# First stage by feature tiles: scale and shift of a tile by partial products in four column quarters, eight output tiles side by side

## The chip, the core and the metric

The kernel runs on one core of a Trainium2 chip. The metric is the device time of one execution in microseconds (us); lower is better. The core has a matrix engine (TensorE: PE in the profile, with PEld for its weight loads), VectorE (DVE), ScalarE (ACT), GpSimd (POOL) and SyncE (SP), which issues the transfers here. Each engine works through its own instructions in order and waits for others by semaphores.

## The reference

Two transformer blocks in float32 for 256 tokens of 1024 features. What the change touches is the beginning of the first block: from the conditioning vectors `c` and `c_ctx` a scale and a shift of each of 1024 features are computed, the tokens `x` and the 256 context tokens `ctx` are normalised, scaled and shifted, and projected by `w_in`.

```python
mod_x = (silu(c) @ w_ada + b_ada)          # 6 parts of 1024: shift, scale, gain of the mixing and of the ffn
mod_c = silu(c_ctx) @ w_ada + b_ada
px = (rms_norm(x,   g_pre_mix) * (1 + sc_m)  + sh_m)  @ w_in
pc = (rms_norm(ctx, g_pre_mix) * (1 + csc_m) + csh_m) @ w_in
# px, pc are split into: attention q, k, v; mLSTM q, k, v, o and 16 gates
# then window attention with a sink, a two-way chunked mLSTM, w_out, residual, SwiGLU;
# a second block of the same size follows, and a last norm
```

## The kernel before, in words

**Layout.** Features lie on the 128 partitions, in KD = 8 feature tiles `k`; tokens lie along the free axis: 256 tokens of `x`, then 256 of `ctx`. A product in float32 is made of three matmuls on rounded halves (`mm3`, L443): high weights by high input, high by low, low by high. H and L are the halves of the weights, `self.xh` and `self.xl` those of the input.

**The weight stream.** `make_plan` (L216) lists all weight blocks of 128 by 128 (320 wide for the values, `v1`) in the order of use and packs them into items of up to 1024 columns. `load_raw` issues one transfer for each into six buffers `raw` (NRAW = 6, L331); a buffer is loaded anew when its item has been split. `prep_item` (L392) splits an item: ACT copies it to H (L399), DVE subtracts to get L (L400). Items of the kind "ada" hold rows of `w_ada` for the later gains; DVE multiplies them by `self.cbx`, the silu of `c` on all partitions (L406), so `cbx` must be there before the first of them. `block()` hands out the next block and keeps the splits LA = 3 items ahead; in the first stage it is 0, and the splits are called by hand.

**The first stage, `start` (L592).** Tokens are loaded, squared on ACT (L657) and summed over the features on DVE (L658); PE sums over the partitions (L527), DVE computes the row factors and lays them on a diagonal (L548), PE spreads them to all partitions (L556), ACT copies them to `R` (L560). The 16 transfers `araw` of 512 KB hold the part of `w_ada` that gives shifts and scales. Scales: `rows(h, i)` multiplies two feature tiles of `cs` (silu of both conditionings, 2 columns) with 512 columns (L673); `scales` turns the two rows into columns (L699) and DVE adds bias and gain (L702, L703). Shifts of tiles 0 to 5: `dots(k)` on DVE (L713) and POOL (L711), summed on ACT (L719); of tiles 6 and 7: `rows_f` (L682) and `shifts` (L692). `inp(k)` applies scale, shift and R to tile k (DVE L727, POOL L728 and L729, ACT L730 and L731), `low(k)` makes the low half (DVE L735, L737).

The run "gates" sends three output tiles of 512 columns (`held`: gates, and two of mLSTM keys) through the eight feature tiles side by side, and the table `hooks` calls `step(k)` and `ahead(k)` between its 24 blocks. Near its end `ahead(5)` issues loads 3 to 5 and beyond and the second part of `cst` (the rotation tables, L793).

**Behind it, `mix1` (L828).** Two tiles of mLSTM queries (`mq`), the attention keys (`ak`) and the first query tile (`aq0`) follow one output tile after another, each over all eight feature tiles; between them the steps of `ml_gates` (log-sigmoid on ACT at L938 to L940, scans on DVE from L943, transposes on PE at L990) are taken by `next(gates)`. Then come the values `v1`, token-major, in two halves of eight blocks; L990 stands between the halves. The string `MIX1` sets the order of what follows: `A` is a unit of attention, `c` of the context state, `q1` to `q3` and `o0` to `o3` are further projections, `a`/`b` the mLSTM heads. PSUM has 8 banks: 4 tagged "mm", 3 "at", 1 "sm".

## Time and profile before

| | |
|---|---|
| time, median of 3 runs | 1040.81 us |
| lowest and highest run | 1036.70 and 1040.88 us |
| span of the profiled execution | 1037.3 us |
| PE busy, share of the span | 994.6 us, 96% |
| DVE, ACT, POOL busy | 663.2, 495.8, 217.5 us |
| bytes moved | 175.56 MB, mean 169 GB/s |

Of the profiled execution its span is recorded, from its first to its last instruction, and no time beside it. Times below count from the start of that span. Busy PE time counts matmuls as they lie in the pipeline, one over the next, so 96% does not mean that PE streams columns 96% of the time.

### The profile page before, as it was taken

The page shows a single profiled execution, that of the slowest core. Times are in us where ns is not written, and L with a number is a line of the kernel's source. Part 1 is how long each engine was busy: PE and PEld are TensorE (multiplying, and loading weights), DVE is VectorE, ACT ScalarE, POOL GpSimd, SP SyncE. Part 2 cuts the span into 40 slices and gives each one's busy share as a digit, 9 for nine tenths or more (in the row PEclk, how much of TensorE's full clock was granted, in tenths as well). Part 3 has the DMA queues.
Part 4 walks back from the last instruction along what each step waited for, and adds up shares of the span by engine and source line. Part 5 has one row for each costly group of instructions (what it writes and reads, how often), then busy time and mean ns, then how long its engine had stood idle before and what let it go on. Part 6 is the DMA issues. An engine that isn't in the chain of part 4 may idle for free. (4 is left out here: it accounts for less than half of the span.)

```text
span 1037.3 us, 18663 instructions
## 1 busy us (share of the span) xinstructions
PE 994.6 (96%) x7500; PEld 917.4 (88%) x7500; DVE 663.2 (64%) x1154; ACT 495.8 (48%) x834; POOL 217.5 (21%) x220
## 2 busy tenths in 40 slices
PE   6899999988999999889999999999999999999996
PEld 2389767888999999789999999998779999999995
DVE  6779758877788744665555554554357866566543
ACT  4374555556544445354444343644355545444441
POOL 0831102360000001411111020115355421111000
PEclk9999999989999999889999999999999999999998
DMA  9665604454678655245555555353224555555531
GB/s 336 239 207 160 207 2 134 175 210 153 203 227 279 205 183 184 81 151 191 168 181 169 174 174 171 102 183 123 82 82 161 185 187 182 188 188 190 184 124 41
DMA packets 49514, 175.56 MB, mean 169 GB/s; under 512 B 5506, under 2 KB 6802, under 8 KB 49428
## 3 DMA queue, kind: packets, MB, share of 16 engines
q1 hardware_dynamic: 49428, 174.38, 50.3%
q8 instruction: 59, 0.97, 0.4%
q14 instruction: 27, 0.22, 0.1%
HBM read 173.30 MB, written 1.05 MB: 168 GB/s over the span
## 5 line engine op out<-in xcount | busy, mean ns | idle before, releaser
L400 DVE TENSOR_TENSOR L<-raw,H 128x1024 fp32r<-128x1024 f32 (+2 forms) x259 | 322.0, 1246 | 224.2 <-ACT H L399 224.0
L399 ACT ACTIVATE H<-raw 128x1024 fp32r<-128x1024 f32 (+2 forms) x278 | 289.7, 1048 | 203.6 <-PE mm L446 83.0
L446 PE MATMUL mm<-x,H 128*128 128x256 f32 (+3 forms) x1064 | 307.6, 289 | 3.9 <-DVE x L737 3.6
L445 PE MATMUL mm<-x,H 128*128 128x256 f32 (+3 forms) x1032 | 301.2, 292 | 3.4 <-ACT x L1249 3.4
L447 PE MATMUL mm<-x,L 128*128 128x256 f32 (+3 forms) x1032 | 297.3, 288 | 0.0
L446 PEld LDWEIGHTS mm<-x,H 128*128 128x128 f32 x1064 | 203.1, 191 | 7.8 <-DVE x L737 5.9
L445 PEld LDWEIGHTS mm<-x,H 128*128 128x128 f32 x1032 | 197.2, 191 | 11.1 <-ACT x L1249 4.8
L447 PEld LDWEIGHTS mm<-x,L 128*128 128x128 f32 x1032 | 196.9, 191 | 1.2
L447 PE MATMUL mm<-hh,L 128*128 128x256 f32 (+1 forms) x528 | 150.3, 285 | 0.0
L445 PE MATMUL mm<-hh,H 128*128 128x256 f32 (+1 forms) x528 | 149.7, 284 | 0.0
L446 PE MATMUL mm<-hl,H 128*128 128x256 f32 (+1 forms) x528 | 149.5, 283 | 0.0
L445 PE MATMUL at<-x,H 128*128 128x256 f32 (+2 forms) x472 | 135.4, 287 | 0.0
L447 PE MATMUL at<-x,L 128*128 128x256 f32 (+2 forms) x472 | 135.3, 287 | 0.0
L446 PE MATMUL at<-x,H 128*128 128x256 f32 (+2 forms) x472 | 135.3, 287 | 0.0
L445 PEld LDWEIGHTS mm<-hh,H 128*128 128x128 f32 x528 | 99.7, 189 | 0.0
L446 PEld LDWEIGHTS mm<-hl,H 128*128 128x128 f32 x528 | 99.5, 188 | 0.0
L447 PEld LDWEIGHTS mm<-hh,L 128*128 128x128 f32 x528 | 99.3, 188 | 0.0
L514 POOL TENSOR_TENSOR acc<-acc,t 128x256 f32<-128x256 f32 (+1 forms) x42 | 41.2, 980 | 238.4 <-ACT t L1206 177.2
L446 PEld LDWEIGHTS at<-x,H 128*128 128x128 f32 x472 | 90.4, 192 | 0.1
L445 PEld LDWEIGHTS at<-x,H 128*128 128x128 f32 x472 | 90.4, 192 | 0.1
L447 PEld LDWEIGHTS at<-x,L 128*128 128x128 f32 x472 | 90.5, 192 | 0.0
L1306 POOL TENSOR_TENSOR g<-g,R 128x272 f32<-128x272 f32 (+1 forms) x44 | 33.2, 758 | 216.7 <-ACT g L1305 216.7
(371 smaller groups left out, 1323.0 us busy)
## 6 DMA issues: line engine op xcount, KB each, us to landing
raw<-wst SPq DMA_DIRECT2D x298, 512.0 KB, 3.8
araw<-ada SPq DMA_DIRECT2D x16, 512.0 KB, 7.5
raw<-wst SPq DMA_DIRECT2D x8, 480.0 KB, 3.4
raw<-wst SPq DMA_DIRECT2D x4, 320.0 KB, 2.8
XT<-xin SPq DMA_DIRECT2D x2, 544.0 KB, 4.3
CT<-cin SPq DMA_DIRECT2D x2, 512.0 KB, 7.5
out<-XT SPq DMA_DIRECT2D x8, 128.0 KB, 2.0
cst<-cst SPq DMA_DIRECT2D x1, 392.0 KB, 4.1
```

The lines of the kernel that those rows point to most:

```text
L399: self.A.activation(H[:, :w], src, AF.Copy)
L400: low = lambda: (self.G if self.poolsplit else self.V).tensor_tensor(L[:, :w], src, H[:, :w].bitcast(F32), op=ALU.subtract)
L445: T.matmul(out, H, xh, start=start, stop=False)
L446: T.matmul(out, H, xl, start=False, stop=False)
L447: T.matmul(out, L, xh, start=False, stop=stop)
L514: self.G.tensor_tensor(st["acc"], st["acc"], sq, op=ALU.add)
L1306: G.tensor_tensor(g, g, R[:, :n], op=ALU.mult)
```

## The change

The first stage goes by feature tiles. One transfer `araw` (1 MB, four buffers) now holds, for feature tile k, the 128 columns of the scale and the 128 of the shift over all eight tiles of the contraction. `mod_rows(k)` multiplies it with `cs`, now 32 columns wide with the two conditionings in the first two: contraction tile j goes to output partitions 32 (j mod 4), so four partial sums grow in four column quarters of the array. ACT copies the 128 by 256 result to `row`. `mod_cols(k)` multiplies it by `sel`, which has ones where the partition modulo 32 is 0 or 1: this adds the quarters and turns rows to columns. `inp(k)` makes M, SH and both halves of the input on DVE and ACT; POOL has no part in it.

Eight output tiles go through the feature tiles side by side: gates, two of mLSTM keys and the attention keys with 512 columns (four "mm" banks), two of mLSTM queries and attention queries 0 and 1 with 256 (two "at" banks, two tiles in each). Query tile 1 thereby moves from `MIX1` to the first stage. `cbx` comes by a transfer that repeats one row for all partitions, and one silu on ACT, behind the stage. The rows of `w_ada` in the stream stand at other places (`ADA1`), as many as before, and the steps of `ml_gates` start with `v1`.

```diff
-    "A c c c q1 c a0 A q2 a1 b0 A a2 A b1 A a3 b2 q3 o0 b3 A t o1 A t t t t t o2 A m t A t k o3 A s"
+    "A c c c a0 A q2 c a1 b0 A a2 A b1 A a3 b2 q3 o0 b3 A t o1 A t t t t t o2 A m t A t k o3 A s"
-ADA1 = (1, 1, 1, 1, 1, 0, 0, 2, 1, 0, 2, 2, 1, 2, 0)
+ADA1 = (1, 1, 1, 1, 1, 1, 1, 1, 2, 2, 1, 2)
+FIRST = (W1_GATES, W1_MK, W1_MK + 128, W1_AK, W1_MQ, W1_MQ + 128, W1_AQ, W1_AQ + 128)
+    put("sel", np.stack([np.arange(128) % 32 == i for i in range(2)], 1).astype(np.float32))
-    add("gates", together([g[:8], g[8:16], g[16:]]))
-    add("mq", w1(W1_MQ, 2))
+    add("first", together([tiles_of("w1", (c // 128,), out=i) for i, c in enumerate(FIRST)]))
...
+            for k in range(4):
+                load_ada(k)
+                self.load_raw(k)
...
+            acc = self.tile(p, [128, 2 * SEQ], "ssq")
             for s, src in enumerate((X, CT)):
+                sq = [self.tile(p, [128, 4, SEQ], f"sq{i}") for i in range(2)]
                 for i, c in enumerate(parts):
+                    A.activation(sq[i], src[:, c], AF.Square)
+                a = sq[0]
+                V.tensor_tensor(a, a, sq[1], op=ALU.add)
+                V.tensor_tensor(a[:, 0:2], a[:, 0:2], a[:, 2:4], op=ALU.add)
+                V.tensor_tensor(acc[:, SEQ * s:SEQ * s + SEQ], a[:, 0], a[:, 1], op=ALU.add)
...
+            def mod_rows(k):
+                for j in range(KD):
+                    g = 32 * (j % 4)
+                    T.matmul(psr[g:g + 32, 0:256], cs[:, j, :], raws[k][:, j, :], start=j < 4, stop=j >= 4)
+                rows[k] = self.tile(p, [128, 256], "row", bufs=2)
+                A.activation(rows[k], psr[:, 0:256], AF.Copy)
+                if k + 4 < KD:
+                    load_ada(k + 4)
+            def mod_cols(k):
+                cols[k] = self.ps("sm")
+                for i in range(2):
+                    T.matmul(cols[k][:, 2 * i:2 * i + 2], rows[k][:, 128 * i:128 * i + 128], self.v("sel"), start=True,
+                             stop=True)
+            def inp(k):
+                ps = cols.pop(k)
+                V.tensor_scalar(M[:, k, :], ps[:, 0:2], b1[:, k:k + 1], self.v("g_pre_mix")[:, k:k + 1], op0=ALU.add,
+                                op1=ALU.mult)
+                V.tensor_scalar(SH[:, k, :], ps[:, 2:4], ba[:, k:k + 1], None, op0=ALU.add)
+                t = self.t2()
+                for s, src in enumerate((X, CT)):
+                    c = slice(SEQ * s, SEQ * s + SEQ)
+                    V.scalar_tensor_tensor(t[:, c], src[:, k, :], M[:, k, s:s + 1], R[:, c], op0=ALU.mult, op1=ALU.mult)
+                    A.activation(self.xh[:, k, c], t[:, c], AF.Identity, bias=SH[:, k, s:s + 1])
                 for s in range(2):
+                    c = slice(SEQ * s, SEQ * s + SEQ)
+                    V.scalar_tensor_tensor(self.xl[:, k, c], t[:, c], SH[:, k, s:s + 1], self.xh[:, k, c].bitcast(F32),
+                                           op0=ALU.add, op1=ALU.subtract)
...
             for k in range(KD):
+                for i, out in enumerate(outs):
+                    H, L = self.block()
+                    c = slice(0, 512 if i < 4 else SEQ)
+                    self.mm3(out, H, L, self.xh[:, k, c], self.xl[:, k, c], k == 0 and (i < 4 or i % 2 == 0),
+                             k == KD - 1 and (i < 4 or i % 2 == 1))
+                    if k == KD - 1:
+                        continue
+                    if i == 0:
+                        mod_rows(k + 1)
+                        self.load_raw(k + 4)
+                    if i == 2:
+                        mod_cols(k + 1)
+                        inp(k + 1)
+                        self.prep_item()
+            self.hold = []
+            for u in range(KD + 3, KD + self.NRAW):
+                self.load_raw(u)
+            S.dma_start(self.cst[:, 128:], self.d["cst"][:, 128:])
+            S.dma_start(self.cbx, self.d["crow"][0:1].to_broadcast([128, D]))
+            A.activation(self.cbx, self.cbx, AF.Silu)
...
+            for c in (2, 3, 0):
+                next(convs[c])
+            for j in range(2):
+                self.rope(hp[2 + j], self.QA[:, j, :])
+            next(convs[1])
+            A.activation(self.KA[:, SEQ:], h[3][:, SEQ:], AF.Copy)
+            self.rope(h[3][:, :SEQ], self.KA[:, :SEQ])
...
             for i, _ in enumerate(self.vproj("v1", (0, 128, 256, 384), ev)):
-                next(gates, None)
+                for _ in range(2 if i < 3 else 1):
+                    next(gates, None)
```

**PE in the middle of the first stage.** Before, with the outputs `mm_261`, `mm_265` and `mm_271` of the run "gates" and `at_352` of `rows_f`:

```order
L445 MATMUL mm_261<-x_7_75,H_302 128x512
L446 MATMUL mm_261<-x_6_74,H_302 128x512
L447 MATMUL mm_261<-x_7_75,L_303 128x512
L445 MATMUL mm_265<-x_7_75,H_302 128x512
L446 MATMUL mm_265<-x_6_74,H_302 128x512
L447 MATMUL mm_265<-x_7_75,L_303 128x512
L682 MATMUL at_352<-araw_239,cs_114 2x256 x4
L682 MATMUL at_352<-araw_244,cs_114 2x256 x4
L445 MATMUL mm_271<-x_7_75,H_302 128x512
```

Of the change, the first blocks of feature tile 1, with `mod_rows(2)` at L640 and `mod_cols(2)` at L650 (the lines here and below are those of the changed kernel):

```order
L432 MATMUL mm_185<-x_7_75,H_226 128x512
L433 MATMUL mm_185<-x_6_74,H_226 128x512
L434 MATMUL mm_185<-x_7_75,L_227 128x512
L640 MATMUL at_133<-araw_94,cs_102 32x256 x8
L432 MATMUL mm_186<-x_7_75,H_226 128x512
L433 MATMUL mm_186<-x_6_74,H_226 128x512
L434 MATMUL mm_186<-x_7_75,L_227 128x512
L432 MATMUL mm_187<-x_7_75,H_226 128x512
L433 MATMUL mm_187<-x_6_74,H_226 128x512
L434 MATMUL mm_187<-x_7_75,L_227 128x512
L650 MATMUL sm_268<-vec_69,row_256 128x2 x2
L432 MATMUL mm_188<-x_7_75,H_226 128x512
```

The products for the scale and shift of tile 2 stand behind the first block of tile 1, and the one that makes columns of them behind the third; one block of 512 columns and four of 256 follow before tile 2 begins.

**ACT at the end of the first stage.** Before (`H` is a split, `x` a high half of the input, `gz` the gates, `t` copies for the convolutions):

```order
L730 ACTIVATE x_7_75<-t_99_422,SH_153 128x256 [waits DVE_49]
L731 ACTIVATE x_7_75<-t_99_422 128x256 [waits Pool_49]
L399 ACTIVATE H_439<-raw_406 128x1024 [waits DMAHW3_49]
L399 ACTIVATE H_447<-raw_408 128x1024 [waits DMAHW4_49]
L848 ACTIVATE gz_471<-mm_261 64x512 [waits DMAHW2_49,DMAHW6_49,DMAHW1_49,DMAHW7_49,DVE_49,Activation_49]
L916 ACTIVATE t_118_482<-mm_265 128x512 [waits PE_49]
```

Of the change, from the last feature tile to the first item of `v1` (`H_650`):

```order
L642 ACTIVATE row_520<-at_133 128x256 [waits PE_49,Activation_49]
L662 ACTIVATE x_7_75<-t_92_535,SH_132 128x256 [waits DVE_49] x2
L386 ACTIVATE H_542<-raw_366 128x1024 [waits DMAHW5_49]
L702 ACT_TABLE_LOAD
L702 ACTIVATE cbx_72<-cbx_72 128x1024 [waits DMAHW5_49]
L751 ACTIVATE gz_603<-mm_185 64x512 [waits DMAHW3_49,DMAHW6_49,DMAHW1_49,DMAHW7_49,DVE_49,Activation_49]
L819 ACTIVATE t_110_614<-at_189 128x256 [waits PE_49]
L819 ACTIVATE t_112_617<-at_189 128x256
L819 ACTIVATE t_114_620<-mm_186 128x512
L819 ACTIVATE t_120_635<-mm_187 128x512
L760 ACTIVATE KA_608<-mm_188 128x256
L386 ACTIVATE H_650<-raw_418 128x960 [waits DMAHW6_49]
```

In each tile the split `H` now stands behind the two halves of the input. At the end the silu of `cbx`, which waits for its transfer, and six copies stand ahead of the split for `v1`; before, the splits of the next items stood ahead of the copies.

**SP at the same place.** Before, around the second part of `cst`:

```order
L389 DMA raw_414<-wst 128x1024 [waits DMAHW7_49,DVE_49]
L389 DMA raw_416<-wst 128x1024 [waits DMAHW0_49,DVE_49]
L793 DMA cst_70<-cst 128x784 [waits DMAHW1_49]
L389 DMA raw_442<-wst 128x960 [waits DMAHW3_49,DMAHW2_49,DVE_49]
L389 DMA raw_451<-wst 128x1024 [waits DMAHW4_49,DVE_49]
```

Of the change (`raw_589` is the sixth load behind the eight of the first stage, into the buffer of the last of them):

```order
L376 DMA raw_587<-wst 128x640 [waits DMAHW4_49,DVE_49]
L376 DMA raw_589<-wst 128x1024 [waits DMAHW5_49,DMAHW3_49,DVE_49]
L700 DMA cst_70<-cst 128x784
L701 DMA cbx_72<-crow 128x1024
L567 DMA csb_598<-csb 128x1152 [waits DMAHW6_49,PE_49]
L376 DMA raw_654<-wst 128x960 [waits DMAHW7_49,DVE_49]
```

`cst` and `cbx` are issued behind a load that waits for the split of the last feature tile's weights.

## Rows read from the trace of the kernel before

**Rows 1.** Page: busy time by engine; groups: count, busy us and mean ns, idle before.

```profile
PE 994.6 (96%) x7500; PEld 917.4 (88%) x7500; DVE 663.2 (64%) x1154; ACT 495.8 (48%) x834; POOL 217.5 (21%) x220
...
L400 DVE TENSOR_TENSOR L<-raw,H 128x1024 fp32r<-128x1024 f32 (+2 forms) x259 | 322.0, 1246 | 224.2 <-ACT H L399 224.0
L399 ACT ACTIVATE H<-raw 128x1024 fp32r<-128x1024 f32 (+2 forms) x278 | 289.7, 1048 | 203.6 <-PE mm L446 83.0
```

**Rows 2.** Windows: stretch, PE, PEld, DVE, ACT, POOL busy (count), PE clock, DMA, GB/s.

```profile
33.00:37.00 4.00, 4.00 (x9) 1.14 (x8) 2.14 (x4) 1.46 (x3) 4.00 (x3) 0.57 1.04 424
...
76.50:90.60 14.10, 14.10 (x98) 13.97 (x96) 13.72 (x24) 3.81 (x4) 4.38 (x5) 1.00 0.56 178
90.60:92.70 2.10, 1.14 (x10) 0.76 (x9) 2.00 (x5) 1.24 (x3) 0.00 (x0) 1.00 0.71 242
```

**Rows 3.** Timeline of the opening: start, duration, engine, line, instruction, idle before.

```profile
7.44 7.44 DVE L658 TENSOR_REDUCE ssq<-prod 128x256 f32<-128x1024 f32 x4 [4.58 <-ACT prod L657]
...
11.25 1.06 ACT L657 ACTIVATE prod<-CT 128x1024 f32<-128x1024 f32 x1 [0.32 <-DVE ssq L658]
...
14.93 0.83 PE L527 MATMUL sm<-ones,ssq 128*128 128x1 f32 x6 [1.43 <-DVE ssq L658]
...
17.09 0.87 DVE L548 TENSOR_SCALAR t<-cst,rs_y 128x128 f32<-128x128 f32 x4
...
20.91 1.12 PE L556 MATMUL sm<-t,ones 128*128 128x512 f32 x2
...
30.10 0.50 PE L445 MATMUL mm<-x,H 128*128 128x512 f32 x1
```

**Rows 4.** Timeline of one feature tile's input, 45 to 47 us.

```profile
45.52 0.17 DVE L702 TENSOR_TENSOR M<-sm,b 128x8 f32<-128x8 f32 x1 [0.19 <-PE sm L699]
...
45.94 0.48 DVE L727 SCALAR_TENSOR_TENSOR t<-XT,M,R 128x256 f32<-128x256 f32 x1
...
46.33 0.48 DVE L735 SCALAR_TENSOR_TENSOR x<-t,SH,x 128x256 fp32r<-128x256 f32 x1
46.45 0.51 ACT L730 ACTIVATE x<-t,SH 128x256 fp32r<-128x256 f32 x1 [1.39 <-DVE t L727]
```

**Rows 5.** Timeline: eight float32 products of 256 columns, plain and in column halves.

```profile
48.24 0.40 PE L447 MATMUL mm<-x,L 128*128 128x512 f32 x1
...
48.56 3.61 PE L682 MATMUL at<-araw,cs 128*2 128x256 f32 x16
...
140.05 1.95 PE L1190 MATMUL at<-PT,AV 128*64 128x256 f32 x16
```

**Rows 6.** Timeline at the end of the run "gates", PE and ACT.

```profile
61.38 0.39 PE L446 MATMUL mm<-x,H 128*128 128x512 f32 x1
61.61 0.39 PE L447 MATMUL mm<-x,L 128*128 128x512 f32 x1
...
62.48 0.59 ACT L848 ACTIVATE gz<-mm 64x512 f32<-64x512 f32 x1 [2.19 <-issue]
...
63.09 1.09 ACT L916 ACTIVATE t<-mm 128x512 f32<-128x512 f32 x2
```

**Rows 7.** Transfers issued from 54 to 62 us: count, KB each, us to landing.

```profile
raw<-wst SPq DMA_DIRECT2D x2, 512.0 KB, 3.5
...
cst<-cst SPq DMA_DIRECT2D x1, 392.0 KB, 4.1
```

**Rows 8.** Timeline: the gates' log-sigmoid (ACT, DVE), the first and last product of `q1`.

```profile
69.09 0.63 ACT L938 ACTIVATE t<-gz 64x512 f32<-64x512 f32 x1 [0.33 <-DVE gz L953]
...
72.98 0.63 ACT L940 ACTIVATE t<-t 64x512 f32<-64x512 f32 x1
...
83.08 0.67 DVE L943 SCALAR_TENSOR_TENSOR gz<-gz,t 64x512 f32<-64x512 f32 x1
...
111.72 0.38 PE L445 MATMUL mm<-x,H 128*128 128x256 f32 x1
...
114.53 0.28 PE L447 MATMUL mm<-x,L 128*128 128x256 f32 x1
```

More of the change, by code (lines that the diff above doesn't have):

```diff
@@ L200, in tiles_of @@
 def tiles_of(key, ms, nk=KD, out=None):
-    return [(key, k, 128 * m, 128, (out or key, j), k == 0, k == nk - 1) for j, m in enumerate(ms) for k in range(nk)]
+    return [(key, k, 128 * m, 128, (key if out is None else out, j), k == 0, k == nk - 1) for j, m in enumerate(ms) for k in range(nk)]
 def stagger(tiles, last=1):
@@ L635, in start @@
-            for _ in range(8):
-                load()
-            cs = self.tile(p, [128, KD, 2], "cs")
             A.activation(cs[:, :, 0], self.v("c"), AF.Silu)
             A.activation(cs[:, :, 1], self.v("cc"), AF.Silu)
-            psr, prods, xs = {}, {}, {}
-            tiles = [(128 * i, 128) for i in range(4)]
-            cb = self.tile(p, [128, D], "cb")
-            cbs = (self.cbx, cb)
-            pick = self.t2(SEQ).rearrange("p (s m) -> p s m", s=2)
-            V.memset(pick, 0.0)
@@ L685, in row_of @@
-            def row_of(h, n=512):
-                row = self.tile(p, [2, D], "crow")
-                A.activation(row[:, :n], psr[h][0:2, :n], AF.Copy)
-                return row
-            def shifts(row, ps):
-                for k in range(2):
-                    T.transpose(ps[:, 2 * k:2 * k + 2], row[0:2, 128 * k:128 * k + 128], self.ident[0:2, 0:2])
-                V.tensor_tensor(SH[:, 6:8], ps[:, 0:4].rearrange("p (k s) -> p k s", s=2),
-                                ba[:, 6:8].unsqueeze(2).to_broadcast([128, 2, 2]), op=ALU.add)
@@ L742, in start @@
-            rows(0, 1)
-            R = self.bcast(r, tiles, dg, out=self.tile(p, [128, 2 * SEQ], "R1"))
-            rows(0, 2)
-            rows(0, 3)
-            for k in range(2):
-                dots(k)
-                dots_end(k)
+            psr = self.ps("at")
+            rows, cols, pend = {}, {}, {}
+            def mod_rows(k):
[6 more added lines that the diff above has]
+                    load_ada(k + 4)
@@ L749, in start @@
+            tiles = [(128 * i, 128) for i in range(4)]
+            r = self.stat_end(dict(tiles=tiles, parts=[acc]), True)
+            mod_rows(0)
+            dg = self.diag(r, tiles)
             self.la = 0
             self.hold = [None]
-            self.fill(1)
-            scales(0, row_of(0), self.ps("mm"))
+            self.prep_item()
+            R = self.bcast(r, tiles, dg, out=self.tile(p, [128, 2 * SEQ], "R1"))
+            mod_cols(0)
             inp(0)
-            dots(2)
-            rows(1, 0)
@@ L797, in start @@
-            hooks = {}
-            for k in range(KD):
-                hooks[3 * k] = lambda k=k: step(k)
-                hooks[3 * k + 2] = lambda k=k: ahead(k)
-            hooks[3 * 4 + 1] = lambda: shifts(row_of(2, 256), self.ps("sm"))
-            self.run("gates", self.xin, slice(0, 512), lambda out, ps: self.held.append(ps), hooks)
+            main = [self.ps("mm") for _ in range(4)]
+            pairs = [self.ps("at") for _ in range(2)]
+            outs = [m[:, 0:512] for m in main] + [q[:, SEQ * i:SEQ * i + SEQ] for q in pairs for i in range(2)]
```

180 lines of the change are left out of this document (27 added, 153 removed).

## The prediction

> **What bounds the kernel now.** I read the page first. PE is busy for 96% of the span, and the splits of the weights are the largest work of DVE and ACT [rows 1]. A share over the whole span says little of a stage of 60 us, so I cut the beginning into windows. From 76.5 us the values `v1` run without a gap, then PE stands between the two halves of `v1`: 1.14 us busy in 2.1 us [rows 2]. Ahead of that the timeline shows a slow start: the sums of squares end at 14.9 us, the row factors lie on their diagonal at 17.96 us, PE spreads them at 20.9 us, and the first matmul of the projections stands only at 30.1 us [rows 3]. The scales and shifts are what it waits for. Behind `v1` PE is so full that I take a shift of `v1` to be a shift of the end. So the question is one of two dates: when `v1` begins (76.5 us), and when its second half begins (92.7 us, 16.2 us later).
>
> **Prices.** A matmul of 512 columns follows the last one after 0.23 us [rows 6], so a block of three is 0.69. The 24 matmuls of `q1` fill 111.72 to 114.65 us, 0.12 each and 0.37 a block [rows 8]. A feature tile has four blocks of each kind: 2.76 + 1.46 = 4.22 us of PE.
>
> `mod_rows` is eight float32 products of 256 columns, 16 passes. Plain, they took 3.61 us; in two column halves, 1.95 us [rows 5]. Four quarters are in no row. If the step is repeated they take 1.0 us; the bounds are 1.0 and the plain 3.61. I take 1.0, being nearest to the halves' law, and it includes the change from one kind of product to the other, 48.56 - 48.24 - 0.23 = 0.09 us [rows 5]. `mod_cols` is four passes with full weight loads; six such passes took 0.83 us [rows 3], so 0.55.
>
> The halves share all 128 rows of the array, and yet ran at nearly twice the plain pace [rows 5]. The Trainium skill (TensorE: Matmul & The Clock Gate, Part 3: Packing small matmuls — row/col tiling) says that a weight load passes under a running matmul only where the two use different row groups. By that rule the quarters would gain nothing, and the sum would be that of the third rival below.
>
> **The step of the new first stage.** What stands behind `mod_cols` of the next tile, counted from its end? From the rows of one tile's input [rows 4]: M starts after 0.03; the first scaled half at 0.25, the second at 0.64 (DVE follows itself after 0.39), ending at 1.12; ACT makes the high halves at 0.76 and 1.16, ending at 1.67. Only then does the split of the tile's weights come, since the order has H behind the two high halves on ACT, and L behind the low halves on DVE: H from 1.6 to 2.65, L (1.25 by [rows 1]) to 3.9 us. PE meanwhile has one block of 512 and four of 256, 2.15 us, and the two matmuls of the next tile that need no L, 0.46. Then it waits. The circle closes through PE: last matmul of the first block 0.23, `mod_rows` 1.0, two blocks 1.38, `mod_cols` 0.55, chain 3.9. **One step: 7.05 us**, where PE's own work is 4.22 + 1.0 + 0.55 = 5.77. DVE and ACT are idle for a part of each step; it is the order of a chain that costs, not their load.
>
> **The opening.** The last square of `ctx` ends at 12.3 us [rows 3]. Three additions of 1024, 512 and 256 elements in place of a reduction (1.25 by [rows 1], then about 0.7 and 0.45 by size) end at 14.7, where the reductions ended at 14.9: a gain of 0.2, so the diagonal ends at 17.75. `mod_rows(0)` lies in the shadow of that. Broadcast 1.12 to 18.85, `mod_cols(0)` to 19.4; the first L holds DVE to 19.7. The tile's low half is there 2.2 us later, then two matmuls 0.46 and 2.93 of PE: the second `mod_cols` ends at 25.3. The granted clock was 0.57 in 33 to 37 us (mostly the lower of its two levels, 1.2 GHz), where PE had nine matmuls in 4 us [rows 2]; before 21.5 us PE will be as sparse. At half speed the first step's 3.6 us would double; I add 1.5, between 0 and 3.6: 26.8. Six more steps: 69.1. The last L is ready at 73.0, and PE ends the stage at 73.0 + 0.23 + 2.07 + 1.46 = 76.8 us.
>
> **From the stage to `v1`.** On SP, `cst` and `cbx` stand behind a load that waits for that last L. One load of 512 KB landed after 3.5 us, `cst` alone after 4.1 [rows 7]. Three together are 1.44 MB; at the 424 GB/s of [rows 2] they move in 3.4 us, and what one load takes beyond its bytes is 3.5 - 1.25 = 2.25. So `cbx` lands 5.6 us after the issue (bounds: 4.1 and the three in a row, 11.1), at 78.6. ACT waits for it in order. Behind the wait are queued: the silu 1.05, six copies out of PSUM (0.6 for `gz`, 1.1 for two of 512 by [rows 6], by size half of one of these for each of three of 256: 2.5), and only then H of the first item of `v1`, 1.0: 83.1. L follows on DVE to 84.3, and `v1` needs it at its second matmul. **`v1` begins as if at 84.2 us, 7.7 later than before**, and PE stands for some 7.4 us. Before, the splits for what followed stood ahead of the copies, so no such gap is seen.
>
> **Between the halves of `v1`.** The log-sigmoid ran on ACT from 69.1 to 73.6 us, long ahead of the DVE part at 83.1 [rows 8]. Now it stands behind four splits, and the fourth needs a load into the buffer that the first L frees at 84.3: landing 3.5 later, H 1.0, then 4.5 us of ACT: 93.3. From the DVE part to the end of the stand took 92.7 - 83.1 = 9.6 us; one more row of the stream (1.22) stands in it now: 104.1. That is 19.9 us behind the start of `v1` in place of 16.2: **3.7 us more**. A slow clock at the start of `v1` disappears in this wait.
>
> **`q1`.** Its 24 matmuls leave the path behind `v1`: 2.9 us by [rows 8]. They gave PE work while the first softmax ran, so a part may return as a wait; bounds 0 and 2.9, I take 2.2. Its split goes too, and one more row of `w_ada` of the same price comes into that phase, so DVE there is even. The bytes are the same, and four tiles are loaded ahead: 1.5 MB in 7 us is half of what the queue moved in 33 to 37 us [rows 2], so no step waits for a transfer.
>
> **Sum.** 7.7 + 3.7 - 2.2 = 9.2 us: the span goes from 1037.3 to 1046.5. The median of the runs shown is 3.5 above that span, with runs on both sides of it; added to the median the forecast is **1050 us**.
>
> **The rivals.**
> First, PE sets the step (the one on the other side: not slower). If the chain behind `mod_cols` were below 2.15 + 0.46 = 2.6 us, a step would cost 5.77; six steps save 7.7 us: 1042.3, no change that a measurement tells. For it: DVE and ACT have room, and POOL no longer works beside DVE. Against it: the splits' place in the order, with 1.05 and 1.25 of [rows 1]. If `cbx` were early as well, it would be 1038.
> Second, `cbx` is there in time. Then the copies wait only for the "at" bank's products, at 76.1; five copies 1.9 remain behind that, H 1.0 and L 1.2: 80.2, 4 us less: 1046. It decides if the transfer lands by about 74.5, under 2 us after its issue; no row has that, but a landing in between gives a part.
> Third, the quarters don't run side by side. Only in pairs: 0.95 more in seven steps, 1057. One after another: 2.6 more, 1068. The halves' row speaks against the second. It is what the skill's rule on row groups, named above, would do here.
>
> **Chances and range.** The forecast 0.58, the first rival 0.12, the second 0.17, the third 0.13 (half of it in pairs). The measured spread of this kernel is 0.4%, so about 0.5% can be told from no change: below 1035.6 faster, above 1046.0 slower. Faster takes both of the first two rivals and a warm clock: 0.06. Within: most of the first rival, half of the second and the forecast's lower end (a step of 6.5 us, or `cbx` early): 0.24. Slower 0.70. The range, 1040 to 1060 us, holds the forecast with its unknown clock (1.5 either way), landing (1.5 less to some 5 more) and `q1` (2.2 more), the first two rivals, and the quarters in pairs. The forecast's own range is 1045 to 1056.
>
> **What would show it.** Right: matmuls of the projections from about 21.5 us; steps of 7 us with PE waiting for L of DVE; ACT idle on a transfer from about 73.5 to 78.6 us; `v1` from 84; a stand of some 5 us between its halves, on ACT or DVE. Wrong: `mod_rows` well above 1.0 us; steps near 5.8 us; `v1` directly behind the stage; or stands behind `v1` that shrink by what was lost ahead of it, which my rule of shifts excludes.

## The result and the profile after

The changed kernel takes 1057.1 us (median of 4 runs, 1055.25 to 1057.89) against 1038.76 us (4 runs, 1036.48 to 1040.88) on the same chip: ratio 1.0154, 95% interval 1.0126 to 1.0183 (the quotient of the two medians, 1.0177, lies in it). The profiled execution has a span of 1055.9 us, 18.6 more than before. The forecast was 9.2 us more; its 1050 stood on the earlier median of 1040.81, and on the 1038.76 of these runs it would be 1048. The sign and the places are as forecast, the size is half of what came.

The page and the windows, as in [rows 1, 2]. The windows are those of the stand ahead of `v1`, its first 6 us, the rest of its first half, the stand between the halves, and the second half (columns: PE, PEld, DVE, ACT, POOL busy with counts, granted clock, DMA share, GB/s):

```profile
PE 990.6 (94%) x7586; PEld 922.2 (87%) x7586; DVE 644.8 (61%) x1150; ACT 493.5 (47%) x829; POOL 197.1 (19%) x200
82.40:90.00 7.60, 0.00 (x0) 0.00 (x0) 2.40 (x10) 4.47 (x9) 3.19 (x5) 0.75 0.28 105
90.00:96.00 6.00, 4.84 (x17) 4.50 (x18) 6.00 (x9) 2.21 (x3) 5.92 (x2) 0.50 0.49 134
96.00:108.40 12.40, 12.40 (x85) 12.12 (x84) 9.35 (x19) 7.33 (x9) 3.40 (x4) 0.98 0.58 212
108.40:111.60 3.20, 0.76 (x6) 0.54 (x6) 3.08 (x7) 1.34 (x3) 0.00 (x0) 1.00 0.83 270
111.50:126.20 14.70, 14.70 (x102) 14.50 (x101) 14.38 (x28) 9.07 (x23) 0.00 (x0) 1.00 0.54 183
```

DVE, ACT and POOL have less to do than before, and PE's work is the same; the loss is not work. PE stands 7.6 us with nothing at all, in a stretch where no engine is full, and 2.44 of the 3.2 us between the halves of `v1`.

The opening, as in [rows 3] (start, duration, engine, line, instruction, idle before):

```profile
15.48 1.93 PE L640 MATMUL at<-araw,cs 128*32 128x256 f32 x16
17.91 2.04 PE L543 MATMUL sm<-t,ones 128*128 128x512 f32 x2 [0.49 <-ACT row L642]
23.55 0.79 PE L432 MATMUL mm<-x,H 128*128 128x512 f32 x1 [1.90 <-ACT x L662]
25.22 1.94 PE L640 MATMUL at<-araw,cs 128*32 128x256 f32 x16
29.05 0.50 PE L650 MATMUL sm<-vec,row 128*128 128x2 f32 x4
```

The projections begin at 23.55 us, 6.5 ahead of before, where 21.5 was forecast. The broadcast takes 2.04 us where it took 1.12, and `mod_rows` 1.93 where it takes 1.07 a step later: until about 28 us PE needs twice the time, as it would at the lower of its two clock levels (1.2 GHz). That it is the clock can't be read from the trace, whose column of the granted clock shows 1.00 there; but with PE kept busy ahead (an experiment below) the same instructions take the short times. The second `mod_cols` is done at 29.55, forecast 26.8.

One step of the stage, to be read beside [rows 4]:

```profile
41.48 1.07 PE L640 MATMUL at<-araw,cs 128*32 128x256 f32 x16
43.98 0.50 PE L650 MATMUL sm<-vec,row 128*128 128x2 f32 x4
44.52 0.28 DVE L655 TENSOR_SCALAR M<-sm,b,vec 128x2 f32<-128x2 f32 x1 [3.52 <-PE sm L650]
45.35 0.91 ACT L662 ACTIVATE x<-t,SH 128x256 fp32r<-128x256 f32 x2 [2.29 <-DVE t L661]
46.17 1.04 ACT L386 ACTIVATE H<-raw 128x1024 fp32r<-128x1024 f32 x1
47.24 1.22 DVE L387 TENSOR_TENSOR L<-raw,H 128x1024 fp32r<-128x1024 f32 x1 [0.46 <-ACT H L386]
47.26 0.50 PE L432 MATMUL mm<-x,H 128*128 128x512 f32 x1 [0.56 <-ACT H L386]
48.52 0.49 PE L434 MATMUL mm<-x,L 128*128 128x512 f32 x1 [0.52 <-DVE L L387]
48.95 1.07 PE L640 MATMUL at<-araw,cs 128*32 128x256 f32 x16
```

From `mod_rows` to `mod_rows` it is 7.47 us, the same in each step. DVE idles 3.52 us for `mod_cols`; then M, the halves of the input, H, L follow one another, and PE waits twice, for H and for L. The sixteen passes that took 3.61 us plain and 1.95 in halves [rows 5] take 1.07, and PE's next matmul starts 1.00 after their start.

The end of the stage and the beginning of `v1` (the place of [rows 6]):

```profile
77.11 1.22 DVE L387 TENSOR_TENSOR L<-raw,H 128x1024 fp32r<-128x1024 f32 x1 [0.46 <-ACT H L386]
78.36 0.33 SPq L376 DMA_DIRECT2D raw<-wst  x1
79.22 0.42 SPq L701 DMA_DIRECT2D cbx<-crow  x1
85.51 1.06 ACT L702 ACTIVATE cbx<-cbx 128x1024 f32<-128x1024 f32 x1 [7.13 <-DMA cbx<-crow]
88.94 2.55 ACT L386 ACTIVATE H<-raw 128x960 fp32r<-128x960 f32 x3
90.60 1.14 DVE L387 TENSOR_TENSOR L<-raw,H 128x960 fp32r<-128x960 f32 x1
90.03 0.64 PE L432 MATMUL at<-H,x 128*128 128x320 f32 x1 [7.66 <-ACT H L386]
91.79 0.64 PE L433 MATMUL at<-L,x 128*128 128x320 f32 x1 [1.12 <-DVE L L387]
```

The transfers issued there, beside [rows 7] (count, KB, us from issue to landing):

```profile
raw<-wst SPq DMA_DIRECT2D x1, 512.0 KB, 3.7
cbx<-crow SPq DMA_DIRECT2D x1, 512.0 KB, 6.3
cst<-cst SPq DMA_DIRECT2D x1, 392.0 KB, 4.3
```

ACT stands for `cbx` with the six copies and the splits of `v1` queued behind it. The second matmul of `v1`, the first that needs L, is at 91.79 us; before it was at 76.64.

The gates, beside [rows 8]:

```profile
95.29 1.00 ACT L386 ACTIVATE H<-raw 128x960 fp32r<-128x960 f32 x1 [3.79 <-DMA raw<-wst]
96.20 0.61 ACT L841 ACTIVATE t<-gz 64x512 f32<-64x512 f32 x1
110.73 0.33 PE L893 MATMUL sm<-cst,gz 64*128 64x64 f32 x2 [2.28 <-ACT gz L883]
```

The log-sigmoid begins at 96.2, behind a split that waited for its load, and PE stands for the gates' columns.

**Where the 18.6 us arose.** Four marks on PE, in each trace: the second matmul of `v1`, the first of its second half, the first of the score products behind it, and the first matmul of the ffn (258 columns). Before:

```profile
76.64 0.31 PE L446 MATMUL mm<-L,x 128*128 128x320 f32 x1
92.66 0.42 PE L445 MATMUL mm<-H,x 128*128 128x320 f32 x1
107.38 1.12 PE L1175 MATMUL mm<-KA,QA 64*128 64x512 f32 x2
222.20 0.58 PE L445 MATMUL mm<-x,H 128*128 128x258 f32 x1 [1.70 <-ACT x L1249]
```

After (the first mark, 91.79, is shown above):

```profile
111.46 0.41 PE L432 MATMUL at<-H,x 128*128 128x320 f32 x1
126.18 1.12 PE L1078 MATMUL mm<-KA,QA 64*128 64x512 f32 x2
239.30 0.58 PE L432 MATMUL mm<-x,H 128*128 128x258 f32 x1 [1.51 <-ACT x L1152]
```

So 15.15 us were lost ahead of `v1`, 3.65 between its halves, nothing in the second half; 1.7 came back up to the ffn, where `q1` is gone; and behind the mark 1.5 were lost again. They lie in the ffn, behind the sums for its norm: there PE had stood 3.43 us, where it was 2.61 before, and the granted clock was at 0.50 within 1 us of the sums (from 257 us), where before it fell 2.5 us behind them (0.80 in 241 to 242, then 0.50).

This is one execution. The last experiment below changes only the order of `mod_rows`' products, and its steps take 7.49 us; its marks are 91.13, 110.66, 126.91 and 239.33, and its span is 1054.3. There 1.5 us are lost in the second half of `v1`, 2.4 come back up to the ffn, and behind the ffn nothing is lost (PE stood 2.63 us ahead of the sums). So the losses ahead of the second half belong to the change; the 1.5 us behind the ffn do not belong to it as such.

### The profile page after: what moved, and what is told of

Its sections match the earlier page's. It is cut to its first block, busy times and chain, and to the rows that moved or that the text cites. A ratio compares the mean times of both kernels' runs of the same rounds, so it can differ in the third digit from the quotient of the medians.

```text
span 1055.9 us, 18783 instructions
## 1 busy us (share of the span) xinstructions
PE 990.6 (94%) x7586; PEld 922.2 (87%) x7586; DVE 644.8 (61%) x1150; ACT 493.5 (47%) x829; POOL 197.1 (19%) x200
## 5 line engine op out<-in xcount | busy, mean ns | idle before, releaser
L387 DVE TENSOR_TENSOR L<-raw,H 128x1024 fp32r<-128x1024 f32 (+1 forms) x259 | 321.0, 1241 | 222.0 <-ACT H L386 221.9
L386 ACT ACTIVATE H<-raw 128x1024 fp32r<-128x1024 f32 (+1 forms) x278 | 289.5, 1047 | 202.3 <-PE mm L433 81.8
L432 PE MATMUL mm<-x,H 128*128 128x256 f32 (+3 forms) x1008 | 296.4, 294 | 9.1 <-ACT H L386 3.9
L433 PE MATMUL mm<-x,H 128*128 128x256 f32 (+3 forms) x1040 | 300.8, 289 | 0.1
L434 PE MATMUL mm<-x,L 128*128 128x256 f32 (+3 forms) x1008 | 291.5, 289 | 3.7 <-DVE L L387 3.7
L432 PEld LDWEIGHTS mm<-x,H 128*128 128x128 f32 x1008 | 192.9, 191 | 17.7 <-ACT H L386 5.4
L433 PEld LDWEIGHTS mm<-x,H 128*128 128x128 f32 x1040 | 198.8, 191 | 1.8 <-DVE x L1154 0.8
L434 PEld LDWEIGHTS mm<-x,L 128*128 128x128 f32 x1008 | 192.6, 191 | 7.9 <-DVE L L387 6.7
L432 PE MATMUL at<-x,H 128*128 128x256 f32 (+2 forms) x496 | 142.2, 287 | 0.0
L433 PE MATMUL at<-x,H 128*128 128x256 f32 (+2 forms) x496 | 141.9, 286 | 0.0
L434 PE MATMUL at<-x,L 128*128 128x256 f32 (+2 forms) x496 | 141.9, 286 | 0.0
L432 PEld LDWEIGHTS at<-x,H 128*128 128x128 f32 x496 | 95.0, 192 | 0.4
L433 PEld LDWEIGHTS at<-x,H 128*128 128x128 f32 x496 | 95.0, 192 | 0.4
L434 PEld LDWEIGHTS at<-x,L 128*128 128x128 f32 x496 | 94.8, 191 | 0.0
```

The lines of the kernel that those rows point to most:

```text
L386: self.A.activation(H[:, :w], src, AF.Copy)
L387: low = lambda: (self.G if self.poolsplit else self.V).tensor_tensor(L[:, :w], src, H[:, :w].bitcast(F32), op=ALU.subtract)
L432: T.matmul(out, H, xh, start=start, stop=False)
L433: T.matmul(out, H, xl, start=False, stop=False)
L434: T.matmul(out, L, xh, start=False, stop=stop)
```

## The experiments

Each was run beside the kernel before, whose medians there were 1038.5 to 1040.4 us; the times are medians, and the ratios, to the kernel before, are to be held against the changed kernel's 1.0154 (1.0126 to 1.0183). The intervals of the split first, of all four and of the two kernels with early gates lie clear of it. Those of the others touch it or overlap it: there the gain is read from marks in one trace each. In the traces of the changed kernel and of the four experiments that alter nothing up to there, the second `mod_cols` starts between 29.05 and 30.05 us, so a difference of up to 1 us in the marks says little.

**The transfer early.** My theory was that the waits ahead of `v1` pass to the end; the rival that the work behind is bound otherwise.

```diff
+            S.dma_start(self.cst[:, 128:], self.d["cst"][:, 128:])
+            S.dma_start(self.cbx, self.d["crow"][0:1].to_broadcast([128, D]))
             for u in range(KD + 3, KD + self.NRAW):
                 self.load_raw(u)
-            S.dma_start(self.cst[:, 128:], self.d["cst"][:, 128:])
-            S.dma_start(self.cbx, self.d["crow"][0:1].to_broadcast([128, D]))
```

> The transfers of cst and cbx are issued ahead of loads 11 to 13 instead of behind them. My theory: in the changed kernel ACT stood 7.13 us for cbx, with the copies and the splits of v1 queued behind it; cbx now is issued at about 63 us and lands long before 77. ACT goes on after the last split with the silu (table load and 1.06) to 79.4, the copies then wait for the last products of the 'at' banks (82.4 us) and end at 84.6, the first H of v1 at 85.6, its L at 87.3 where it was 91.74. All behind it shifts by the same 4.4 us: 1052.7 us. Rival A: the copies and the rotation behind them, and not cbx, set the split (they wait for the end of the stage's products), so v1 moves by under 2 us: 1055 or more. Rival B: v1 moves by 4.4 us, but the work behind is bound elsewhere (loads, DVE) and stands grow: 1056 to 1057.

1052.1 us (ratio 1.0127, 1.0094 to 1.016). The silu runs straight behind the last split, at 79.39 us, and the second matmul of `v1` is at 87.57, 4.2 earlier. The theory holds for `cbx`. But the second half, 4.3 us earlier at its beginning, is only 2.8 earlier at its end:

```profile
107.10:123.40 16.30, 16.30 (x103) 16.08 (x101) 15.98 (x30) 9.23 (x23) 0.00 (x0) 0.90 0.62 200
```

It takes 16.3 us at a mean clock of 0.90, where the changed kernel took 14.7 at 1.00. The first of the ffn is 3.6 earlier, and the slow start of the ffn is not there; so the span is 5.6 us shorter.

**The split first.**

```diff
                     if i == 0:
+                        self.prep_item()
                         mod_rows(k + 1)
                         self.load_raw(k + 4)
                     if i == 2:
                         mod_cols(k + 1)
                         inp(k + 1)
-                        self.prep_item()
```

> The split of the next tile's weights (H, L) is called behind the first block of a tile, ahead of the scales and the input, instead of behind them. My theory: the chain behind mod_cols loses H and L (2.3 us) and falls below PE's own work; a step goes from 7.47 to 5.8 us, seven steps gain 10 to 11.5 us, the last L is no longer late; the rest (cbx, copies, the stand between the halves of v1) stays as long as it is and only moves: 1046 us. Rival A: the steps are paced by something else (loads of w_ada, the copy of the row, the clock), steps stay above 7 us and the time at 1054 or more. Rival B: the stage ends 11 us earlier, but cbx and the loads behind the last split move by less, so that the stand ahead of v1 grows: about 1050.

1042.65 us (ratio 1.0038, 1.001 to 1.0067): 14.5 us less, more than the 11 expected. Two rows of the copy behind `mod_rows` in following steps, the last matmul ahead of a `mod_rows`, and the silu:

```profile
57.74 0.38 ACT L642 ACTIVATE row<-at 128x256 f32<-128x256 f32 x1 [1.48 <-PE at L640]
63.76 0.38 ACT L642 ACTIVATE row<-at 128x256 f32<-128x256 f32 x1 [1.48 <-PE at L640]
62.24 0.39 PE L434 MATMUL mm<-x,L 128*128 128x512 f32 x1
69.46 1.06 ACT L702 ACTIVATE cbx<-cbx 128x1024 f32<-128x1024 f32 x1 [0.81 <-DMA cbx<-crow]
```

A step is 6.02 us, and from one `mod_rows` to the next (56.54 to 62.56 us) PE is busy in all of it: PE itself now sets the step. And ACT waits only 0.81 us for `cbx`: the load ahead of it on SP needs the last split of the stage, which now comes a tile earlier, so one edit took both delays. The second matmul of `v1` is at 76.33 us, where it was before the change. This is the largest cause.

**The first split of `v1` ahead of the silu.**

```diff
+            self.prep_item()
             A.activation(self.cbx, self.cbx, AF.Silu)
```

> The first item of v1 is split right behind the last split of the first stage, ahead of the silu of cbx on ACT; cbx stays late. My theory: PE gets a first block of v1 at about 82.3 us, and the following ones as the copies free the banks from 87.2 us; in sum v1 is some 4.5 us ahead. The fourth split's load is issued 12 us earlier, so that the log-sigmoid no longer waits for it and ends 4 us earlier: 1052.5 us. Rival: the copies out of PSUM are what v1 waits for (banks), and the gates' chain, which needs the same copies, does not move: 1056 to 1057.

1055.3 us (ratio 1.0152, 1.012 to 1.0184); the time alone tells no gain. The second matmul of `v1` is 9.4 us earlier, but the next ones wait for banks (3.78 us for `gz`); the second half begins at 107.7, 3.8 earlier, and takes 17.3 us at a clock of 0.83, so that 1.2 of it are left behind `v1` and 1.6 at the ffn. The chain of the gates did move, against the rival; the slow second half took most of it.

**The log-sigmoid behind three splits.**

```diff
             next(gates)
+            self.la -= 1
             for i, _ in enumerate(self.vproj("v1", (0, 128, 256, 384), ev)):
                 for _ in range(2 if i < 3 else 1):
                     next(gates, None)
+                if i == 0:
+                    self.ahead(1)
```

> The log-sigmoid of the gates stands on ACT behind three splits of v1 instead of four; the fourth waits for a load. My theory: it begins at 91.6 instead of 96.2 us, the scans on DVE move with it, and the stand of 2.3 us between the halves of v1 goes; PE's slow clock at the start of v1 comes to light, so of the 4.5 us some 3 are gained: 1054 us. Rival: the chain of the gates is set by DVE (splits and rows of w_ada between its steps), so the stand shrinks by under 1 us: 1056.5.

1054.8 us (ratio 1.0159, 1.0123 to 1.0196); here too the time alone tells no gain. The log-sigmoid begins at 91.53 us, and the second half at 109.4 in place of 111.46: PE's wait for the gates' columns is 0.16 us. The clock stays at 1.00 in the second half (14.7 us), and the first matmul of the ffn is 2.5 us earlier. By the marks the theory holds, with 2 to 2.5 us where I had said 3.

**All four.**

> The four edits together (transfers of cst and cbx ahead of loads 11 to 13; split ahead of the input; first split of v1 ahead of the silu; log-sigmoid behind three splits). In the trace with the split first alone, PE ended the first stage at 72.1 us and got the first L of v1 at 76.3, and the second half of v1 began at 95.9. My theory: v1 now runs from about 72.3 us; but the gates' chain starts only some 3.5 to 4.5 us earlier, so that the second half begins at 92 and PE stands between the halves for 5 to 7 us; what is gained against the split alone is the chain's shift: 1038 to 1039.5 us. Rival A: the time follows the start of v1, 4 us and the stand's slow clock: 1036. Rival B: the edits gain nothing beside the split, since it made cbx early already: 1042 to 1043.

1040.0 us (ratio 1.0001, 0.9978 to 1.0025). The second matmul of `v1` is at 70.77, yet its second half begins at 93.07: PE stands 6.3 us for the gates' columns, as expected, and then runs slow (16.7 us at 0.86). The time lies between the theory and rival B, and the interval overlaps that of the split alone. The differences of the single medians from 1057.1, 5 and 14 and 2 and 2 us, don't add: the transfer's is within that of the split, and what is won ahead of `v1` is waited for between its halves. A part of that wait came from POOL, whose additions ran long beside DVE (the last section): the scans wait for a field that is cleared behind them.

```profile
82.99 0.68 DVE L866 TENSOR_TENSOR_SCAN gB<-ones,gz 4x256 f32<-4x256 f32 x1 [1.09 <-POOL gB L856]
```

**The gates' steps spread.**

```diff
             for i, _ in enumerate(self.vproj("v1", (0, 128, 256, 384), ev)):
-                for _ in range(2 if i < 3 else 1):
-                    next(gates, None)
+                next(gates, None)
```

> On the changed kernel alone: one step of the gates behind each block of v1, not two behind the first three, so that the transposes of the gates stand behind the twelfth block on PE and not behind the eighth or ninth. My theory: the stand between the halves (PE idle from 108.45 to 110.73 us and 0.16 more) is only the place of the transposes in PE's order; 3 us behind, the chain is done and PE does not stand: 1054 us, with the L of v1's first block still at 91.7. Rival: the chain on DVE slows with its steps, or what needs the gates' columns (the context state, first heads) stands instead: 1056 to 1058.

1061.4 us (ratio 1.0215, 1.0179 to 1.0251): slower, outside both. PE no longer stands at the transposes, but here:

```profile
113.99 1.28 ACT L876 ACT_TABLE_LOAD   x1 [7.74 <-DVE gsm L874]
115.29 0.51 ACT L876 ACTIVATE gz<-gi,gsm 64x256 f32<-64x256 f32 x1
115.97 0.20 ACT L767 ACTIVATE AV<-at 128x64 f32<-128x64 f32 x1
116.22 0.63 PE L432 MATMUL at<-H,x 128*128 128x320 f32 x1 [5.92 <-ACT AV L767]
```

The second half needs a bank of the first, and the copies that free it stand on ACT behind the exponential of the gates, which waits for DVE; there ten operations of the convolutions had come between two pairs of scans. My theory that the stand is only the transposes' place on PE falls: with the steps at either of the two places PE waits for the chain, each time by another engine's order.

**Query tile 1 back.** `FIRST` of seven tiles, `q1` again in `MIX1`; first with the items of eight blocks as they were, then with items of seven, one feature tile each (the last line).

```diff
-FIRST = (W1_GATES, W1_MK, W1_MK + 128, W1_AK, W1_MQ, W1_MQ + 128, W1_AQ, W1_AQ + 128)
+FIRST = (W1_GATES, W1_MK, W1_MK + 128, W1_AK, W1_MQ, W1_MQ + 128, W1_AQ)
-    add("first", together([tiles_of("w1", (c // 128,), out=i) for i, c in enumerate(FIRST)]))
+    add("first", together([tiles_of("w1", (c // 128,), out=i) for i, c in enumerate(FIRST)]), (), (7,))
```

> On the changed kernel: query tile 1 goes back to its place behind v1, the first stage has seven output tiles. My theory: in the first stage PE waits for the chain, so that the four... eight blocks of query tile 1 lie in the shadow of it; without them a step loses only what H and L are shorter (896 for 1024 columns, some 0.27 us), 1.6 us in six steps and 0.4 at the end, while 24 matmuls come back behind v1 (2.9 us, and up to 3.6 by the shift of the first head): 1058 to 1059 us. Rival: the tile behind v1 filled a wait and costs nothing there: 1055.

> Query tile 1 goes back behind v1 as in the run before, but now the items of the first stage are seven blocks, one feature tile each; in the run before they stayed eight blocks, so that each split came a block earlier against its use and left the chain, and that run measured the split too. My theory: with whole tiles the split stands in the chain again; a step is 7.47 less 0.27 us (H and L are 896 wide), 1.9 us in all, and the 24 matmuls come back behind v1 for 2.9 to 3.6: 1058 to 1059 us. Rival: query tile 1 costs as much in the first stage as behind v1, by the copies, the rotation and its split: 1055.

The first took 1048.5 us (ratio 1.0092, 1.0056 to 1.0127), against all expectation: its steps are 6.02 us. With items of eight blocks each split comes a block earlier against its use, so the split leaves the chain as in the second experiment. It measured that once more, and not `q1`. The second, with the chain as it was (steps of 7.23 us), took 1058.9 us (ratio 1.0179, 1.014 to 1.0218), in the range of the theory, though the times alone don't tell it from the changed kernel. Its trace, of its slowest execution (1064.85), has the first score product 0.3 us ahead of the changed kernel's and the first of the ffn 2.4 behind. By these marks `q1` is worth some 2.8 us at its place, and a part of that was lost in the first stage by the wider splits.

**PE kept busy in the opening.** 48 products of ones, never read: 36 ahead of the sums, then 4, 2 and 6.

```diff
+            spin(36)
             tiles = [(128 * i, 128) for i in range(4)]
...
             mod_rows(0)
+            spin(4)
...
+            spin(2)
             mod_cols(0)
+            spin(6)
```

> On the changed kernel: 48 products of a tile of ones, written to a free bank and never read, keep PE busy in the opening (36 ahead of the sums, then 4, 2 and 6 in the gaps). In the changed kernel the first two mod_rows took 1.93 us against 1.07 later, the broadcast 2.04 against 1.12, mod_cols 1.01 against 0.50, all at a granted clock of half. My theory: with the clock at 1.00 the second mod_cols ends at about 26.7 us instead of 29.55; the stage and all behind it shift by 2.5 to 3: 1054.3 us. Rival A: the granted clock does not rise by these products, and they only delay PE: 1057 to 1058. Rival B: the opening is bound by DVE and ACT, and a fast PE gains under 1 us: 1056.5.

1057.7 us (ratio 1.0184, 1.0149 to 1.0218): no change. The opening did what the theory said (though the half clock that I named for it is wrong as a reading: the clock's column shows 1.00 there, and only the durations are doubled), and the rest did not:

```profile
22.04 0.50 PE L432 MATMUL mm<-x,H 128*128 128x512 f32 x1 [0.47 <-ACT x L662]
25.72 0.50 PE L650 MATMUL sm<-vec,row 128*128 128x2 f32 x4
108.80:125.50 16.70, 16.70 (x101) 16.51 (x100) 16.38 (x31) 9.05 (x23) 0.00 (x0) 0.87 0.62 195
```

The second `mod_cols` starts 3.3 us earlier; to within about 1 us that is the price of the slow opening. `v1` is 4.15 earlier, its second half 2.65; but this half now runs at 0.87 and takes 16.7 us, so that 0.67 are left at its end and 0.15 at the ffn.

**The gates early, and then with a busy opening.** The second experiment's edit; `cst` and `cbx` issued at the fourth tile and the silu at the seventh; the first split of `v1` behind the stage; and in `mix1`:

```diff
             A.activation(self.gz, h[0][64:128, :], AF.Copy)
+            gates, ctxs = self.ml_gates(), self.ml_ctx()
+            next(gates)
+            for _ in range(2):
+                self.prep_item()
...
+            for _ in range(2):
+                self.prep_item()
             next(gates)
+            self.prep_item()
+            lows = []
+            self.prep_item(lows)
+            self.la -= 1
             for i, _ in enumerate(self.vproj("v1", (0, 128, 256, 384), ev)):
                 for _ in range(2 if i < 3 else 1):
                     next(gates, None)
+                if i == 2:
+                    lows.pop()()
+                if i == 3:
+                    self.ahead(1)
```

> The split ahead of the input, cst and cbx issued in the fourth tile, the silu of cbx in the seventh, the first split of v1 ahead of all copies, the gates' bias behind their copy, the log-sigmoid behind the other copies and the third split of v1, and the fourth split's low half behind the scans. With the four simple edits together PE had v1 from 70.4 us and stood 1.4, 2.7 and 2.2 us between its halves, for the gates' columns; the log-sigmoid ended at 78.4, the scans began at 83. My theory: the scans now begin at about 78.5 us, the last columns are there at 86 to 87 instead of 92.5, PE stands for 1 to 3 us in all and its clock holds better: 1034 us against 1040. Rival A: the stand goes over to the splits of the second half of v1 (loads, DVE), time 1038 to 1040. Rival B: PE's clock falls all the same behind the stand and what is gained ahead is lost by it: 1037.

> The kernel with the early gates, and the products of ones in the opening. On the changed kernel these products brought the second mod_cols from 29.05 to 25.7 us, but the clock fell to half from 106 to 114 us and nothing was left at the end. My theory: with a short stand between the halves of v1 the 3.3 us pass on: 3 us less than the kernel with the early gates. Rival: the clock falls behind v1 again and takes 2 us or more of it back: within 1 us of that kernel.

1035.6 us (ratio 0.9957, 0.993 to 0.9984) and 1035.4 us (0.9953, 0.9927 to 0.9978): both beat the kernel before, by some 0.4%. In the first PE has `v1` from 71.9 us, stands 0.5 and 2.7 us at the transposes and begins the second half at 89.1:

```profile
87.76 0.34 PE L909 MATMUL sm<-cst,gz 64*128 64x64 f32 x2 [2.70 <-ACT gz L893]
```

The scans began at 81.2 us instead of the expected 78.5, since DVE's rows of `w_ada` took up to 1.76 us there in place of 1.21; the total lies between the theory and its second rival. The busy opening puts the first score product 2.2 us ahead of that, and of these 0.8 are left at the ffn; in the medians no difference can be told. Its rival is right.

**The order of the quarters.** `mod_rows` with its products in another order, in one execution.

```diff
-                for j in range(KD):
+                for j in (0, 4, 1, 5, 2, 6, 3, 7):
                     g = 32 * (j % 4)
```

> On the changed kernel mod_rows takes its eight products in the order 0, 4, 1, 5, 2, 6, 3, 7, so that two products for the same quarter follow each other. In the changed kernel a mod_rows of 16 passes takes 1.07 us, which is 0.067 a pass where a plain pass takes 0.226. My theory: the passes of one quarter follow each other slowly and only different quarters run side by side, so that mod_rows takes about 1.5 to 2 us, and each of the seven steps, in which PE's mod_rows lies in the chain, is longer by as much: span up by 3 to 6 us. Rival: the order has no part in it, mod_rows stays at 1.07 and the span at 1056.

```profile
33.13 1.09 PE L640 MATMUL at<-araw,cs 128*32 128x256 f32 x16
```

1.09 us in place of 1.07, span 1054.3: the rival is right. Two products for one quarter in a row cost next to nothing; more in a row were not tried. So passes with 32 columns of weights go at 0.07 us in either order; that they go because they use different quarters is not shown.

## Why the prediction was right in its direction and half in its size

**What held.** The change loses by order, not by work: ACT idle on `cbx`, the splits behind the input, the log-sigmoid behind four splits. The chain from `mod_cols` to L was forecast at 3.9 us and `mod_cols` itself at 0.55; together they are 43.98 to 48.46, 4.48 for 4.45. `mod_rows` was taken at 1.0 by the halves' pace and is 1.0 to PE's next matmul, so the third rival falls. By the rule of the Trainium skill (TensorE: Matmul & The Clock Gate, Part 3: Packing small matmuls — row/col tiling) that a weight load passes under a matmul only with another row group, sixteen passes over all rows should have taken the plain 3.61; the trace does not agree. Between the halves of `v1` I had 19.9 us from its start; they are 111.46 - 91.79 + 0.13 = 19.8. The slow clock at the start of `v1` (0.50 until 96 us) disappears in that wait, as forecast; it leaves 2.44 us of stand where some 5 were named. `q1` was put at 2.2 of its 2.9; 1.7 were left at the ffn, and 2.4 in the trace with the other order of the quarters.

That 1057.1 lies in the range of 1040 to 1060 is in part luck. It is above the forecast's own 1045 to 1056, where the range was held open for the quarters in pairs (1057), and that did not come about.

**What was mis-sized** is the term "from the opening to `v1`", 7.7 us forecast, 15.15 measured. It has four parts.
- *The opening*: I added 1.5 for the slow clock, between 0 and 3.6; with PE kept busy the second `mod_cols` came 3.3 earlier, so the upper end was near. In all it is 2.75 late; some 0.9 of that is left with PE kept busy (26.22 for the 25.3 of the sum before the 1.5).
- *The step*: 7.47 for 7.05, six times, 2.5 us. Chain and `mod_cols` are right; what failed is PE's part behind L, 0.23 + 1.0 + 1.38 forecast. From 48.52 to the next `mod_cols` (51.45) it is 2.93: the last matmul ahead of `mod_rows` holds PE 0.43 and the first behind it 0.34, where I had 0.23 for each. With the split first, where PE does not wait, the one ahead holds it 0.32 (62.24 to 62.56) and the one behind 0.34. So the change of kind costs some 0.1 at either end; the other 0.1 ahead is that this matmul stands behind a wait, as the one at 47.26 does, which holds PE 0.34 with no change of kind.
- *The transfer*: `cbx` lands 7.1 us after the load ahead of it was issued (78.36 to 85.5), not 5.6. It is issued 0.86 us behind that load, and from its own issue it takes 6.3 against 4.3 for `cst`.
- *From the silu to L*: 6.2 us (85.5 to 91.74) for 5.7. DVE had the gates' bias, queued behind the rotation of the keys, ahead of L.

2.75 + 2.5 + 1.5 + 0.5 make 7.25, against 15.15 - 7.7 = 7.45; the rest is in the roundings of the chain. Of the span's +18.6 that leaves 1.5 for the slow start of the ffn, which no term had and which the trace with the other order of the quarters does not have.

**The rivals.** The first was priced with PE's 5.77 us a step; with the split out of the chain a step is 6.02 and PE is busy in all of it, so that its mechanism is right and its price 0.25 short, for the most part at the changes of kind. Its gain, 14.5 us, is larger than the 7.7 priced, because the steps had been longer than forecast and the early split frees the load that holds `cbx`. That the experiment's 1042.65 is so near to the 1042.3 said for this rival is luck. The second, `cbx` in time, was put at 4 us less; in the medians it is 5, at the ffn 3.6.

**The rule of shifts** ("a shift of `v1` is a shift of the end") holds for the trace of the changed kernel, and three experiments (the early transfer, the first split of `v1`, the busy opening) fall short of it by 1.5 to 2.6 us in the second half of `v1`, which took 16.3 to 17.3 us at a clock of 0.83 to 0.90 in place of 14.7 at 1.00. But the trace with the other order of the quarters has such a half too (16.1 us at 0.89), with nothing won ahead of it. So the comparison leans on one execution that kept its clock, and how much of a gain the slow half takes back is not shown. The rule should have been given bounds by what such a half costs.

## What to carry to other kernels

Where a tile's input is made just ahead of its use, put the work that hangs on no result (the split of the next weights) ahead of it on each engine's queue; here that was worth 14 of the 18 us, a part of them because it freed the transfer's issue too. A transfer whose only reader is far away can still stop an engine, if its first reader stands in that engine's order ahead of urgent work: trace both what its issue waits for and what is queued behind its arrival. Price a chain to the next stand and not only to the next stage: an earlier start is worth what the following stand lets through; what the clock behind that stand adds differs between executions.

## What the runs showed of the hardware beside that

The granted clock behind stands of like length was not the same. In the trace of the changed kernel PE was at half clock (0.50) from 90 to 96 us, stood 2.44 us in all at 108 to 111, and kept 1.00 behind it. With the other order of the quarters PE's history was nearly the same (0.50 from 90 to 94 us, a stand of 2.47 us in all), and behind it the clock was 0.74 in 110 to 114 us and 0.83 in 114 to 118:

```profile
109.93 0.34 PE L893 MATMUL sm<-cst,gz 64*128 64x64 f32 x2 [2.32 <-ACT gz L883]
110.00:114.00 4.00, 3.85 (x20) 3.67 (x21) 3.82 (x9) 3.98 (x12) 0.00 (x0) 0.74 0.26 104
```

In the experiment with the early transfer the stand was as long (2.31 us at its longest), ahead of it PE was at 0.50 only from about 88 to 91 us, and behind it the mean clock was 0.57 over 108 to 112. What decides it no run here tells.

An addition on POOL of 256 columns took 0.73 us, and 8.18 us when DVE ran splits and rows of `w_ada` back to back:

```profile
89.66 0.73 POOL L834 TENSOR_TENSOR t<-t,cst 128x256 f32<-128x256 f32 x1 [3.44 <-DVE t L832]
90.47 8.18 POOL L835 TENSOR_TENSOR KA<-t,t 128x256 f32<-128x256 f32 x1
```

It ended 0.6 us behind the last of them. The Trainium skill (GPSIMD Engine Reference, 1. Specifications) says that POOL shares its interfaces to SBUF with VectorE, and that the two contend where a DVE instruction reads two inputs from SBUF; the splits do, and the trace agrees. Nothing on the path waited for this one, but the gates' fields are cleared behind it on POOL, and with all four edits the scans waited 1.09 us for that.
